# Transposing the gated FFN products by the DMA crossbar in 16-bit halves instead of on TensorE

## The chip, the cores and the metric

The kernel runs on one core of one Trainium2 chip. The metric is the device time of one execution in microseconds (us). A core has five engines with instruction streams of their own: TensorE (PE in the profile, with its weight loads as PEld), VectorE (DVE), ScalarE (ACT), GpSimd (POOL) and SyncE (SP), which here issues nearly all transfers. Sixteen DMA rings move the data.

## The reference

An encoder trunk of two layers on a sequence of 256 tokens with 1024 features in float32. Each layer is a half-step FFN, a mixing block with two attention branches, and a second half-step FFN:

```python
def swiglu(x, w_gate, w_up, w_down):
    return (jax.nn.silu(x @ w_gate) * (x @ w_up)) @ w_down

for l in range(DEPTH):                                   # 2
    x = x + 0.5 * swiglu(rms_norm(x, ffn1_norm[l]), ffn1_w_gate[l], ffn1_w_up[l], ffn1_w_down[l])
    ...                                                  # attention branches, gates, output projection
    x = x + 0.5 * swiglu(rms_norm(x, ffn2_norm[l]), ffn2_w_gate[l], ffn2_w_up[l], ffn2_w_down[l])
```

The hidden width D_FF is 2816. The change touches only the four FFNs: the gated product silu(x @ w_gate) * (x @ w_up) has tokens on the partitions when it is made, and must have the hidden features on the partitions to be multiplied by w_down.

## The kernel before

All 256 tokens stay on the chip, as two tiles of 128 tokens (t = 0 and 1). Every float32 product is made of three matmuls (`three`, lines 169 to 172): each operand is split by `split_to` (lines 183 to 185) into a high part, copied by ScalarE into a rounded format, and a low part, the difference, subtracted by VectorE; high times high, high times low and low times high are summed in PSUM.

**Weights.** SP loads them in pieces of 512 KB into four `raw` buffers (line 142, and line 348 for the down weights). ScalarE and VectorE split each piece into one of six pairs `wh`, `wl`, from which TensorE reads. A piece of an up stage serves four groups of three matmuls.

**The up stage of an FFN.** The hidden width is cut into eleven chunks of 256 columns (`for c in range(NFC)`). For each chunk four pieces of the gate and up weights are loaded, and for each of the two token tiles eight groups of three matmuls (`project`) fill a PSUM bank `g`, of which there are two: 256 columns of gate and 256 of up. Then `glu` (lines 440 to 445) applies silu on ScalarE (line 443) and multiplies on VectorE (line 444) into `hh`, a float32 tile of 128 tokens x 2 x 256. In some chunks (`PREP`, three in each FFN) `prepare` also loads two rows of down weights and forms their differences u and v, which it keeps in split form.

**The transposes.** Chunks are collected in pairs. A pair's `turn` (lines 315 to 322) is deferred until TensorE has done some more matmuls (`H_LAG`, `LAST_LAG`; `defer`, `tick` and `need` hold this list by hand), and then issues four transposes of 128x128 per chunk on TensorE through the identity, into a PSUM bank `tp` (line 320). `arrange` takes it from there. `PLAN` gives each chunk a letter. For S (three chunks), `split_to` reads PSUM and gives `hi` and `lo` of four blocks. For F and G (eight chunks), ScalarE copies PSUM to a tile `a` (line 330), VectorE forms four sums of blocks (line 333), and `split_to` gives seven blocks: these are the operands of a multiplication of 2x2 blocks with seven products in place of eight.

**The down stage.** `down` goes through the chunks in order: for F and G seven groups of three matmuls, whose weights are sums and differences of blocks (`differences`, line 352, unless prepared), for S eight. Chunk 0 comes first; chunks 9 and 10, both S, come last and together.

**Order.** TensorE's instructions are issued in the order of the program, which is fixed by hand with the deferrals. On the other engines and on SP's queue a planner fixes an order when the kernel is built, by priority (the order in the program) and by its own estimate of when each instruction becomes ready; on the chip each engine then follows that order and waits where something is not there.

**Buffers that the change shares.** Tag `xg` has two buffers, used by `hh` and by small tiles of the norms; tag `sums` has two of 4 KB per partition, used by `a`, by the differences `u` and `v`, and by the sums at the end of the down stage.

Of the kernel before, what the change touches and what calls it, by code (L numbers as in the profile page):

```python
# [11 lines left out]
F32 = mybir.dt.float32  # L12
F32R = mybir.dt.float32r
I32 = mybir.dt.int32
BF16 = mybir.dt.bfloat16
AF = mybir.ActivationFunctionType
ALU = mybir.AluOpType
AX = mybir.AxisListType
# [3 lines left out]
P = 128  # L22
# [4 lines left out]
T = S // P  # L27
KD = D // P
FC = 256
NFC = FF // FC  # L30
# [13 lines left out]
H_LAG, NORM_LAG, QK_LAG, P_LAG, V_LAG, M_LAG = 7.9, 4.0, 16, 10, 7.5, 5.5  # L44
LAST_LAG = 6.1
# [13 lines left out]
def hybrid_encoder(ctx, tc, x, w_gu1, w_d1, w_in, b_gate, qk_gain, rpb, sink, t5,  # L59
                   w_bna, w_bsw, w_out, w_gu2, w_d2, c_mask, c_band, out):  # L60
    nc = tc.nc
# [3 lines left out]
    act = ctx.enter_context(tc.tile_pool(name="act", bufs=1))  # L65
# [3 lines left out]
    ps_tp = ctx.enter_context(tc.tile_pool(name="ps_tp", bufs=2, space=PSUM))  # L69
# [18 lines left out]
    ident = const.tile([P, P], F32, name="ident")  # L88
# [5 lines left out]
    warm = const.tile([P, 1], F32, name="warm")  # L94
    warmed = nc.scalar.activation(warm, ident[:, :1], AF.Silu)
    qkg = const.tile([P, L, 4], F32, name="qkg")
# [27 lines left out]
    def linked(engine, emit):  # L124
        with ExitStack() as order:
            if engine in chain:
                order.enter_context(tc.issue_after(chain[engine].ins))
            inst = emit()
        if chain:
            chain[engine] = inst  # L130
        return inst
# [13 lines left out]
    def columns(w, l, c0, n, nk=KD):  # L145
        return [load(w[l, 2 * i * P:(2 * i + 2) * P, c0:c0 + n].rearrange("(k p) n -> p k n", p=P), 2, n)
                for i in range(nk // 2)]
# [7 lines left out]
    def defer(lag, key, fn):  # L155
        later.append((now[0] + lag, len(later), key, fn))
        later.sort(key=lambda e: e[0])

    def need(*keys):
        for e in [e for e in later if e[2] in keys]:  # L160
            later.remove(e)
            e[3]()
# [20 lines left out]
    def split_to(hi, lo, src):  # L183
        linked("act", lambda: nc.scalar.activation(hi, src, AF.Copy))  # L184
        linked("dve", lambda: nc.vector.tensor_tensor(lo, src, hi.bitcast(F32), ALU.subtract))  # L185
# [3 lines left out]
    rstd = [None] * T  # L189
# [3 lines left out]
    def norm(t, n, half, apart=False):  # L193
# [9 lines left out]
        if apart and half == 1:  # L203
            for i in range(4):
                linked("act", lambda: nc.scalar.activation(xg[:, i, :], tp[:, i, :], AF.Copy,
                                                           scale=gain[:, n, 4 + i:5 + i]))
# [7 lines left out]
    def square(t, half, junk=None):  # L214
        if junk is None:
            junk = act.tile([P, 512], BF16, name="junk", tag="xg", bufs=2)
        linked("act", lambda: nc.scalar.activation(junk, xs[t][:, half * 512:(half + 1) * 512], AF.Square,
                                                   accum_out=ssq[t][:, half:half + 1]))
# [6 lines left out]
    def opening(w, l, early):  # L225
        def piece(i, c=0):
            return load(w[l, 2 * i * P:(2 * i + 2) * P, c * 512:(c + 1) * 512].rearrange("(k p) n -> p k n", p=P),
                        2, 512)

        ps = [ps_g.tile([P, 512], F32, name="g", tag="g") for _ in range(T)]  # L230

        def steps(t, i):
            wh, wl = pieces[i]
            xh, xl = xT[t]
            for a, b in ((xh, wh), (xl, wh), (xh, wl)):
                for k in (2 * i, 2 * i + 1):
                    nc.tensor.matmul(ps[t], a[:, k, :], b[:, k % 2, :], start=a is xh and b is wh and k == 0,
                                     stop=b is wl and k == KD - 1)
            tick(2)

        pieces = []
        chain["act"] = warmed
        warmup(5)
        norm(0, 0, 0, True)
        pieces.append(piece(0))
        warmup(5)
        fetch(1, 0)
        norm(1, 0, 0, True)
        pieces.append(piece(1))
        fetch(0, 1)  # L250
        fetch(1, 1)
        warmup(3)
        steps(0, 0)
        norm(0, 0, 1, True)
        steps(1, 0)
        pieces.append(piece(2))
        norm(1, 0, 1, True)
        pieces.append(piece(3))
        square(0, 0, idle)
        square(0, 1, idle)  # L260
        for i in (1, 2, 3):
            for t in range(T):
                steps(t, i)
        second = [piece(0, 1)]
        square(1, 0, idle)
        early(ps[0])
        second.append(piece(1, 1))
        square(1, 1, idle)
        second += [piece(i, 1) for i in range(2, KD // 2)]
        chain.clear()  # L270
        defer(24, "constants", constants)
        defer(70, "scaled", scaled)
        return ps, second
# [36 lines left out]
    def ffn(l, n, w_gu, w_d, after):  # L310
        with tc.tile_pool(name="ffn", bufs=1) as fp:
            hs = {}
            SLOT = ((1, 2), (0, 3))

            def turn(group):
                tps = [ps_tp.tile([P, 4, P], F32, name="tp", tag="tp") for _ in group]
                for (_, hh), tp in zip(group, tps):
                    for t in range(T):
                        for i in range(2):
                            nc.tensor.transpose(tp[:, SLOT[t][i], :], hh[:, t, i * P:(i + 1) * P], ident)  # L320
                for (c, _), tp in zip(group, tps):
                    arrange(c, tp)

            def arrange(c, tp):
                m = 4 if PLAN[c] == "S" else 7
                hi = fp.tile([P, m, P], F32R, name=f"hi{m}", tag=f"hi{m}", bufs=NS if m == 7 else NFC - NS)
                lo = fp.tile([P, m, P], F32R, name=f"lo{m}", tag=f"lo{m}", bufs=NS if m == 7 else NFC - NS)
                if m == 7:
                    a = fp.tile([P, 8, P], F32, name="a", tag="sums", bufs=2)
                    nc.scalar.activation(a[:, :4, :], tp, AF.Copy)  # L330
                    for to, x, y, op in ((4, 0, 3, ALU.add), (6, 1, 0, ALU.subtract), (5, 4, 1, ALU.subtract),
                                         (7, 2, 5, ALU.subtract)):
                        nc.vector.tensor_tensor(a[:, to, :], a[:, x, :], a[:, y, :], op)
                    split_to(hi, lo, a[:, 1:, :])
                else:
                    with tc.high_priority(150 if c == NFC - 1 else 0):
                        split_to(hi, lo, tp)
                hs[c] = (hi, lo)

            def get(t, k):  # L340
                need(("h", k // 2))
                return [h[:, SLOT[t][k % 2], :] for h in hs[k // 2]]

            stored = {}
# [68 lines left out]
            def combine(acc):  # L413
                p1, p16 = [fp.tile([P, 2, 512], F32, name=n, tag="sums", bufs=2) for n in ("p1", "p16")]
                ends = act.tile([P, 512], F32, name="ends", tag="xg", bufs=2)
                nc.scalar.activation(p1[:, 0, :], acc["1"], AF.Copy, scale=0.5)

# [20 lines left out]

            def glu(t, ps, pair):
                if t == 0:  # L440
                    pair[0] = act.tile([P, T, FC], F32, name="hh", tag="xg", bufs=2)
                sg = fp.tile([P, FC], F32, name="sg", tag="sg", bufs=2)
                linked("act", lambda: nc.scalar.activation(sg, ps[:, :FC], AF.Silu, scale=rstd[t]))  # L443
                linked("dve", lambda: nc.vector.scalar_tensor_tensor(pair[0][:, t], ps[:, FC:], rstd[t], sg,  # L444
                                                                     op0=ALU.mult, op1=ALU.mult))

            waiting = []
            for c in range(NFC):
                first = n == 0 and c == 0
                pair = [None]  # L450
                if first:
                    both, second = opening(w_gu, l, lambda ps: glu(0, ps, pair))
                elif n == 0 and c == 1:
                    pieces = second
                else:
                    pieces = columns(w_gu, l, c * 512, 512)
                prep = PREP if n else PREP_FIRST
                if c in prep:
                    prepare(prep[c])
                for t in range(T):  # L460
                    if not first:
                        glu(t, project(t, pieces, 512), pair)
                    elif t:
                        glu(t, both[t], pair)
                waiting.append((c, pair[0]))
                if c % 2 or c == NFC - 1:
                    defer(LAST_LAG if c == NFC - 1 else H_LAG, ("h", c), lambda group=waiting: turn(group))
                    waiting = []

            down()  # L470

# [373 lines left out]
```

## Time and profile before

| | |
|---|---|
| time, median of 3 runs | 1077.5 us (1076.47 to 1078.26) |
| span of the profiled execution, first to last instruction | 1075.2 us; its own whole time is not listed apart from the three runs |
| granted clock of TensorE, mean | 0.999 |
| TensorE busy | 1068.2 us (99%), 5125 instructions |
| VectorE busy | 875.8 us (81%) |
| ScalarE busy | 671.5 us (62%) |
| GpSimd busy | 116.7 us (11%) |
| DMA | 212.63 MB, 198 GB/s in the mean |

The profile's rows read as follows. A group of instructions has its source line, engine and operation, the tile written and those read, the shape and the count; then the busy time in us and the mean of one in ns; then the time for which the engine stood idle just before them, and what ended that. A row of waits has who waited for whom, the total in us, how many times, and the longest. A window has start and end, its length, then busy time (and number of instructions) of PE, PEld, DVE, ACT and POOL, the granted clock, the DMA rings' busy share and GB/s. A DMA row has the tile, the queue, the count, the size and the median time from issue to landing. Busy times of matmuls overlap at their ends, so a chain of work or the distance between starts tells better what one costs.

### The profile page before, as it was taken

Reading aid. Unit: us, or ns where it says so; the run is one execution under the profiler, and the core shown is the slowest. Engines: PE = TensorE matmul, PEld = TensorE weight load, DVE = VectorE, ACT = ScalarE, POOL = GpSimd, SP = SyncE. Lnnn points to the kernel's source line nnn. Section 1 sums busy time; section 2 is a strip of 40 time slices with the busy share of each in tenths; the row PEclk is TensorE's granted clock in tenths of the full one; section 3 lists DMA queues with packets and bytes.
Section 4 is the critical chain, followed back from the end, with each engine's and each line's share of the span. In section 5 each row is a group of like instructions: output and inputs, shape, how many; then the busy total and the mean of one; then the engine's idle time right before and its main releaser. Section 6 shows DMA issues by size and latency. Waiting matters only on the chain.

```text
span 1075.2 us, 14749 instructions
## 1 busy us (share of the span) xinstructions
PE 1068.2 (99%) x5125; PEld 890.3 (83%) x5125; DVE 875.8 (81%) x1337; ACT 671.5 (62%) x1014; POOL 116.7 (11%) x118
## 2 busy tenths in 40 slices
PE   8999999999999999999999999999999999999998
PEld 6888888888888888888888888888888888888887
DVE  6678799889886768869977887988898867778696
ACT  6566654788764556565565665557877646566552
POOL 1000120243520000000000000003534000000000
PEclk9999999999999999999999999999999999999999
DMA  7767656765654667756657765657666554776652
GB/s 247 227 214 237 215 190 191 228 194 155 192 188 137 198 199 246 242 168 191 214 162 238 227 213 185 199 153 247 177 195 185 176 175 160 237 231 203 188 196 89
DMA packets 98827, 212.63 MB, mean 198 GB/s; under 512 B 7568, under 2 KB 13744, under 8 KB 98752
## 3 DMA queue, kind: packets, MB, share of 16 engines
q1 hardware_dynamic: 98560, 211.60, 62.3%
q8 instruction: 40, 0.66, 0.2%
q14 instruction: 35, 0.29, 0.1%
q0 software_dynamic: 192, 0.08, 0.1%
HBM read 210.59 MB, written 1.06 MB: 197 GB/s over the span
## 4 chain that ended last, share of the span: by engine, by line
PE 97%; DMA 1%; ACT 1%; DVE 0%; issue 0%; SPq 0%; ACTq 0%
PE g L170 22%; PE g L172 22%; PE g L171 22%; PE acc L170 5%; PE acc L172 5%; PE acc L171 5%; PE tp L320 2%; PE sc L568 1%; PE po L603 1%; PE tp L170 1%; PE tp L171 1%; PE tp L172 1%; PE pt L589 1%; PE tp L201 1%; PE br L170 1%; PE br L171 1%
## 5 line engine op out<-in xcount | busy, mean ns | idle before, releaser
L185 DVE TENSOR_TENSOR wl<-raw,wh 128x1024 fp32r<-128x1024 f32 x336 | 405.7, 1219 | 65.5 <-ACT wh L184 61.8
L184 ACT ACTIVATE wh<-raw 128x1024 fp32r<-128x1024 f32 x336 | 346.7, 1045 | 117.3 <-DMA raw<-in_w_gu 51.4
L170 PE MATMUL g<-wh,xh 128*128 128x512 f32 (+1 forms) x976 | 383.1, 393 | 0.5 <-DVE hh L444 0.5
L172 PE MATMUL g<-wh,xl 128*128 128x512 f32 (+1 forms) x976 | 377.8, 387 | 0.0
L171 PE MATMUL g<-wl,xh 128*128 128x512 f32 (+1 forms) x976 | 377.5, 387 | 0.0
L172 PEld LDWEIGHTS g<-wh,xl 128*128 128x128 f32 x976 | 183.4, 188 | 39.1 <-DVE xl L185 1.5
L170 PEld LDWEIGHTS g<-wh,xh 128*128 128x128 f32 x976 | 183.6, 188 | 33.8 <-DVE hh L444 1.1
L171 PEld LDWEIGHTS g<-wl,xh 128*128 128x128 f32 x976 | 183.7, 188 | 33.4 <-DVE wl L185 0.6
L443 ACT ACTIVATE sg<-g,rs_y 128x256 f32<-128x256 f32 x88 | 41.1, 467 | 89.7 <-PE g L172 77.3
L444 DVE SCALAR_TENSOR_TENSOR hh<-g,rs_y,sg 128x256 f32<-128x256 f32 x88 | 42.3, 481 | 53.0 <-ACT sg L443 53.0
L170 PE MATMUL acc<-wh,hi 128*128 128x512 f32 x180 | 71.2, 395 | 0.0
L171 PE MATMUL acc<-wl,hi 128*128 128x512 f32 x180 | 70.2, 390 | 0.0
L172 PE MATMUL acc<-wh,lo 128*128 128x512 f32 x180 | 70.1, 390 | 0.0
L176 POOL TENSOR_TENSOR rs_y<-ms,mhalf 128x1 f32<-128x1 f32 x12 | 8.1, 678 | 556.5 <-DVE ms L222 548.0
L352 DVE TENSOR_TENSOR u<-raw 128x512 f32<-128x512 f32 x64 | 41.7, 686 | 20.9 <-DMA raw<-in_w_d 20.8
L184 ACT ACTIVATE corner<-raw 128x512 fp32r<-128x512 f32 x32 | 20.1, 629 | 40.4 <-DMA raw<-in_w_d 22.4
L581 POOL TENSOR_TENSOR S<-S,sm 128x512 f32<-128x512 f32 x32 | 37.2, 1161 | 65.6 <-DVE sm L580 38.3
L172 PEld LDWEIGHTS acc<-wh,lo 128*128 128x128 f32 x180 | 33.8, 188 | 7.2
L171 PEld LDWEIGHTS acc<-wl,hi 128*128 128x128 f32 x180 | 33.8, 188 | 6.7
L170 PEld LDWEIGHTS acc<-wh,hi 128*128 128x128 f32 x180 | 33.8, 188 | 6.7
L184 ACT ACTIVATE wh<-v 128x1024 fp32r<-128x1024 f32 x20 | 21.2, 1062 | 28.9 <-DVE v L352 24.5
L574 ACT ACTIVATE S<-S,mx 128x256 f32<-128x256 f32 x64 | 31.9, 499 | 8.0 <-DVE mx L571 7.9
(189 smaller groups left out, 1522.0 us busy)
## 6 DMA issues: line engine op xcount, KB each, us to landing
raw<-in_w_gu SPq DMA_DIRECT2D x176, 512.0 KB, 4.5
raw<-in_w_d SPq DMA_DIRECT2D x100, 512.0 KB, 4.2
raw<-in_w_in SPq DMA_DIRECT2D x64, 512.0 KB, 4.7
raw<-in_w_out SPq DMA_DIRECT2D x16, 512.0 KB, 3.6
bb<-in_b_gate SPq DMA_DIRECT2D x16, 256.0 KB, 3.6
raw<-in_w_bsw SPq DMA_DIRECT2D x8, 512.0 KB, 3.9
raw<-in_w_bna SPq DMA_DIRECT2D x8, 512.0 KB, 3.5
raw<-in_w_d SPq DMA_DIRECT2D x12, 256.0 KB, 2.7
```

Source lines behind the costliest of these rows:

```text
L170: nc.tensor.matmul(ps, xh, wh, start=first, stop=False)
L171: nc.tensor.matmul(ps, xh, wl, start=False, stop=False)
L172: nc.tensor.matmul(ps, xl, wh, start=False, stop=last)
L184: linked("act", lambda: nc.scalar.activation(hi, src, AF.Copy))
L185: linked("dve", lambda: nc.vector.tensor_tensor(lo, src, hi.bitcast(F32), ALU.subtract))
L201: nc.tensor.transpose(tp[:, i, :], xs[t][:, k * P:(k + 1) * P], ident)
L320: nc.tensor.transpose(tp[:, SLOT[t][i], :], hh[:, t, i * P:(i + 1) * P], ident)
L352: sub = lambda to, x, y: nc.vector.tensor_tensor(to, x, y, ALU.subtract)
L443: linked("act", lambda: nc.scalar.activation(sg, ps[:, :FC], AF.Silu, scale=rstd[t]))
L444: linked("dve", lambda: nc.vector.scalar_tensor_tensor(pair[0][:, t], ps[:, FC:], rstd[t], sg, op0=ALU.mult, op1=ALU.mult))
L574: nc.scalar.activation(S_[:, t, :], S_[:, t, :], AF.Exp, bias=mx[:, t:t + 1], scale=-1.0, accum_out=sm[:, t:t + 1])
L581: nc.gpsimd.tensor_tensor(S_, S_, sm.unsqueeze(2).to_broadcast([P, T, S]), ALU.mult)
```

## The change

Per chunk, right after its second gated product, without pairing or deferral:

1. `glu` writes its product in the order of the four blocks that the down stage wants (`hh` is 128 x 4 x 128).
2. ScalarE reads `hh` as 16-bit halves and copies them into a tile `z16` so that all low halves stand first and then all high halves (1024 values of 16 bits per partition).
3. One crossbar transpose on SP's queue turns `z16` into `zT`, eight blocks of 128x128 16-bit values, in a `sums` buffer.
4. ScalarE copies `zT` into `a` (a second `sums` buffer) so that the halves are side by side again as float32.
5. For F and G the four sums and the split follow as before; for S the split now reads `a`.

TensorE's transposes, their PSUM banks and the copy of line 330 go, and so do the deferrals of `turn`. The call of `high_priority` for the last chunk's split goes too.

```diff
-            def turn(group):
-                tps = [ps_tp.tile([P, 4, P], F32, name="tp", tag="tp") for _ in group]
-                for (_, hh), tp in zip(group, tps):
-                    for t in range(T):
-                        for i in range(2):
-                            nc.tensor.transpose(tp[:, SLOT[t][i], :], hh[:, t, i * P:(i + 1) * P], ident)
-                for (c, _), tp in zip(group, tps):
-                    arrange(c, tp)
-
-            def arrange(c, tp):
+            def turn(c, hh):
+                z = act.tile([P, 2, 4 * P], U16, name="z16", tag="xg", bufs=2)
+                nc.scalar.activation(z, hh.bitcast(U16).rearrange("p s (n two) -> p two (s n)", two=2), AF.Copy)
                 m = 4 if PLAN[c] == "S" else 7
                 hi = fp.tile([P, m, P], F32R, name=f"hi{m}", tag=f"hi{m}", bufs=NS if m == 7 else NFC - NS)
                 lo = fp.tile([P, m, P], F32R, name=f"lo{m}", tag=f"lo{m}", bufs=NS if m == 7 else NFC - NS)
+                zT = fp.tile([P, 2 * 4, P], U16, name="zT", tag="sums", bufs=2)
+                nc.sync.dma_start_transpose(zT, z.rearrange("p two n -> p (two n)"))
+                a = fp.tile([P, 8, P], F32, name="a", tag="sums", bufs=2)
+                nc.scalar.activation(a[:, :4, :].bitcast(U16).rearrange("p s (n two) -> p two (s n)", two=2),
+                                     zT.rearrange("p (two s) n -> p two (s n)", two=2), AF.Copy)
                 if m == 7:
-                    a = fp.tile([P, 8, P], F32, name="a", tag="sums", bufs=2)
-                    nc.scalar.activation(a[:, :4, :], tp, AF.Copy)
                     for to, x, y, op in ((4, 0, 3, ALU.add), (6, 1, 0, ALU.subtract), (5, 4, 1, ALU.subtract),
                                          (7, 2, 5, ALU.subtract)):
                         nc.vector.tensor_tensor(a[:, to, :], a[:, x, :], a[:, y, :], op)
                     split_to(hi, lo, a[:, 1:, :])
                 else:
-                    with tc.high_priority(150 if c == NFC - 1 else 0):
-                        split_to(hi, lo, tp)
+                    split_to(hi, lo, a[:, :4, :])
                 hs[c] = (hi, lo)
 
             def get(t, k):
-                need(("h", k // 2))
                 return [h[:, SLOT[t][k % 2], :] for h in hs[k // 2]]
...
                 if t == 0:
-                    pair[0] = act.tile([P, T, FC], F32, name="hh", tag="xg", bufs=2)
+                    pair[0] = act.tile([P, 4, P], F32, name="hh", tag="xg", bufs=2)
+                h = pair[0][:, 0::3, :] if t else pair[0][:, 1:3, :]
...
-                waiting.append((c, pair[0]))
-                if c % 2 or c == NFC - 1:
-                    defer(LAST_LAG if c == NFC - 1 else H_LAG, ("h", c), lambda group=waiting: turn(group))
-                    waiting = []
+                turn(c, pair[0])
```

More of the change, by code (lines that the diff above doesn't have):

```diff
@@ L15 @@
 BF16 = mybir.dt.bfloat16
+U16 = mybir.dt.uint16
 AF = mybir.ActivationFunctionType
@@ L440, in glu @@
                 if t == 0:
-                    pair[0] = act.tile([P, T, FC], F32, name="hh", tag="xg", bufs=2)
+                    pair[0] = act.tile([P, 4, P], F32, name="hh", tag="xg", bufs=2)
+                h = pair[0][:, 0::3, :] if t else pair[0][:, 1:3, :]
                 sg = fp.tile([P, FC], F32, name="sg", tag="sg", bufs=2)
                 linked("act", lambda: nc.scalar.activation(sg, ps[:, :FC], AF.Silu, scale=rstd[t]))
-                linked("dve", lambda: nc.vector.scalar_tensor_tensor(pair[0][:, t], ps[:, FC:], rstd[t], sg,
-                                                                     op0=ALU.mult, op1=ALU.mult))
-            waiting = []
+                linked("dve", lambda: nc.vector.scalar_tensor_tensor(
+                    h, ps[:, FC:].rearrange("p (i n) -> p i n", i=2), rstd[t], sg.rearrange("p (i n) -> p i n", i=2),
+                    op0=ALU.mult, op1=ALU.mult))
             for c in range(NFC):
@@ L464, in ffn @@
                         glu(t, both[t], pair)
-                waiting.append((c, pair[0]))
-                if c % 2 or c == NFC - 1:
-                    defer(LAST_LAG if c == NFC - 1 else H_LAG, ("h", c), lambda group=waiting: turn(group))
-                    waiting = []
+                turn(c, pair[0])
             down()
```

## The prediction

> **What bounds the kernel now.** I read the page's busy shares first, then its chain of work that ended last, then TensorE's waits, to see whether TensorE is busy because it works or because it is fed late.
>
> ```profile
> span 1075.2 us, 14749 instructions
> PE 1068.2 (99%) x5125; PEld 890.3 (83%) x5125; DVE 875.8 (81%) x1337; ACT 671.5 (62%) x1014; POOL 116.7 (11%) x118
> ...
> PE 97%; DMA 1%; ACT 1%; DVE 0%; issue 0%; SPq 0%; ACTq 0%
> PE g L170 22%; PE g L172 22%; PE g L171 22%; PE acc L170 5%; PE acc L172 5%; PE acc L171 5%; PE tp L320 2%; PE sc L568 1%; PE po L603 1%; PE tp L170 1%; PE tp L171 1%; PE tp L172 1%; PE pt L589 1%; PE tp L201 1%; PE br L170 1%; PE br L171 1%
> ```
>
> ```profile
> PE idle L120 <- DVE blank L115: 1.6, 1, 1.6
> PE tp L201 <- DMA x<-in_x: 1.3, 1, 1.3
> PE g L170 <- DVE hh L444: 0.5, 1, 0.5
> ```
>
> The chain is 97% TensorE, and TensorE waits for others 3.4 us in all, at the opening. So TensorE's own instructions are the time, and each one taken away is worth its place in the stream. Line 320, the transposes that the change takes off TensorE, has 2% of that chain. What has to be judged is whether the other engines and the queue, which now just hide, still hide. Their room is read from the four stages of gate and up projections (24 to 129, 365 to 480, 546 to 661 and 896 to 1011 us), from a prepared chunk inside one (421 to 433) and from one down stage (480 to 542).
>
> ```profile
> core 0: us, PE busy (x) PEld busy (x) DVE busy (x) ACT busy (x) POOL busy (x), PEclk, DMA share, GB/s
> 24.00:129.00 105.00, 104.54 (x478) 86.57 (x478) 81.89 (x115) 63.06 (x79) 2.52 (x5) 1.00 0.71 231
> 365.00:480.00 115.00, 115.00 (x528) 95.31 (x527) 85.68 (x120) 69.14 (x88) 0.56 (x1) 1.00 0.68 221
> 480.00:542.00 62.00, 62.00 (x282) 51.19 (x281) 58.44 (x78) 35.50 (x45) 0.55 (x1) 1.00 0.56 179
> 546.00:661.00 115.00, 114.96 (x528) 95.30 (x527) 87.25 (x121) 67.66 (x87) 0.93 (x1) 1.00 0.69 222
> 896.00:1011.00 115.00, 115.00 (x528) 95.26 (x528) 85.97 (x120) 68.65 (x88) 0.56 (x1) 1.00 0.69 220
> ...
> 421.00:433.00 12.00, 12.00 (x55) 9.94 (x54) 10.50 (x11) 7.17 (x9) 0.00 (x0) 1.00 0.92 301
> ```
>
> In the gate and up stages ScalarE is busy about 60% and the DMA rings 0.68 to 0.71; in the down stage VectorE has 58.44 of 62 us. Those are the three covers that the change leans on.
>
> **The change, part by part.** First, what goes from TensorE. The chain in order of time shows the transposes as pieces of their own:
>
> ```profile
> 456.20 0.87 PE tp L320 x8
> 478.85 0.87 PE tp L320 x8
> 489.95 0.44 PE tp L320 x4
> ```
>
> A pair of chunks with its eight transposes takes 22.65 us (478.85 less 456.20). It has 96 matmuls of 512 columns, so a matmul takes (22.65 - 0.87)/96 = 0.227 us of the stream and a group of three 0.68. One of the four FFNs has 44 transposes, five groups of eight and one of four: 5 x 0.87 + 0.44 = 4.79 us, and four FFNs 19.2 us. I take the pieces of the chain, not the busy time of the group below (23.1 us), for that counts ends that overlap the next matmul. A chunk's period goes from 11.33 to 10.89 us; that is the budget for everything else.
>
> ```profile
> L320 PE MATMUL tp<-ident,hh 128*128 128x128 f32 x176 | 23.1, 272 | 0.0
> L184 ACT ACTIVATE wh<-raw 128x1024 fp32r<-128x1024 f32 x328 | 342.1, 1055 | 116.7 <-DMA raw<-in_w_gu 51.4 <-PE g L172 37.4 <-PE acc L172 11.6
> L330 ACT ACTIVATE a<-tp 128x512 f32<-128x512 f32 x32 | 17.9, 593 | 0.0
> L443 ACT ACTIVATE sg<-g,rs_y 128x256 f32<-128x256 f32 x88 | 41.1, 467 | 89.7 <-PE g L172 77.3 <-issue 12.0 <-PE g L237 0.3
> L444 DVE SCALAR_TENSOR_TENSOR hh<-g,rs_y,sg 128x256 f32<-128x256 f32 x88 | 42.3, 481 | 53.0 <-ACT sg L443 53.0
> L184 ACT ACTIVATE hi<-tp 128x512 fp32r<-128x512 f32 x12 | 7.2, 597 | 1.0 <-PE tp L320 1.0
> ```
>
> ScalarE gets two copies per chunk, one that separates 1024 halves per partition and one that joins them. The nearest row by elements is the weight split of 1024 values, 1.055 us. No row reads or writes 16-bit values at a stride: I bound one copy by 0.6 us (512 words, the L330 row) and by 2.1 us (twice the split), and take 1.055, whose element count it has. It loses the 593 ns copy on the 32 chunks of plans F and G. Net 44 x 2.11 - 32 x 0.593 = 73.9 us, 1.68 per chunk. Now ScalarE has 69.14 x 11.33/115 = 6.81 us of work in a chunk's period; it will have 8.49 of 10.89, and 2.4 us stay free. With the upper bound it would have 10.6, still under the period but with nothing left for waits. VectorE keeps the same instructions: the gated products go to another layout in the same 128x256 size, and the low halves of the three S chunks read SBUF in place of PSUM. I cost that at nothing; VectorE's free quarter in the up stages is the cover.
>
> The rings and SP. Each chunk adds one transpose of 256 KB between parts of SBUF, 44 in all, on SP's queue among the weight loads.
>
> ```profile
> q1 hardware_dynamic: 98560, 211.60, 62.3%
> ...
> q0 software_dynamic: 192, 0.08, 0.1%
> ...
> raw<-in_w_gu SPq DMA_DIRECT2D x176, 512.0 KB, 4.5
> raw<-in_w_d SPq DMA_DIRECT2D x100, 512.0 KB, 4.2
> raw<-in_w_in SPq DMA_DIRECT2D x64, 512.0 KB, 4.7
> ...
> raw<-in_w_d SPq DMA_DIRECT2D x12, 256.0 KB, 2.7
> ...
> raw<-in_w_in SPq DMA_DIRECT2D x8, 256.0 KB, 3.8
> ```
>
> Ring time now: 0.69 x 11.33 = 7.8 us per chunk, so 10.89 leaves 3.1. A load's packet is 211.60 MB/98560 = 2147 bytes and takes 0.623 x 1075.2 x 16/98560 = 0.109 us of one ring. Lower end: the transpose at the same rate per byte is 262144/2147 = 122 packets, 0.83 us of all sixteen rings. Upper end: a row of 128 two-byte values is 256 bytes, so 1024 rows, each at the full 0.109 us (the q0 row, 0.1% for 192 packets of some 420 bytes, says that a short packet is hardly cheaper), 7.0 us. I take 1.5 us, what 512 KB costs more to landing than 256 KB of the same tensor (4.2 against 2.7), because the byte count is the same; then the rings are 9.3 of 10.89 us busy and the loads still hide. The Trainium skill, "DMA: Bandwidth & Descriptors", section "Latency and other measured facts", has crossbar transposes at 261 GB/s in one kernel, which by estimate is 1.0 us here; the sum by it is the same, and no run before shows it.
>
> ```profile
> SPq L142 <- DVE wl L185: 437.1, 195, 8.3
> ...
> L142 SPq DMA_DIRECT2D raw<-in_w_gu x176: 367/368/567, 1.2 to 995.4; - x176
> ...
> ACT wh L184 <- DMA raw<-in_w_gu: 51.4, 51, 2.4
> ```
>
> SP issues a load in 0.37 us and mostly stands waiting for a raw buffer. The transpose's issue lies between 0.33 and, at four times as many rows, 1.5 us: hidden. But it waits in SP's order for ScalarE's first copy, with the next weight loads queued behind it, and itself stands behind loads that wait for a buffer. Behind those loads wait ScalarE's splits, then TensorE; the cover is the six pairs of weight buffers, each worth 4 x 0.68 = 2.72 us of TensorE. Loads that are late already stop ScalarE by at most 2.4 us and TensorE never, so I cost this at nothing; uncovered, it costs what the rival on ScalarE's order costs.
>
> The path of one chunk: silu 0.47, product 0.48, separation 1.06, transpose 2.7 to 3.8 to landing, joining 1.06, then the high and low parts. It ends some 9 us after the chunk's last matmul. Nothing in the up stage reads it; the down stage starts with chunk 0 and comes to chunks 9 and 10 last. The latency itself is hidden. The banks that the transposes used on TensorE come free earlier; that earns nothing, as TensorE never waits for them. What the path holds are two buffers "sums", shared with the differences of the down weights, and two "xg". For xg, the separation ends 2.0 us after the chunk and the next product comes 5.4 us after it: hidden. For "sums" the last chunk counts. The timelines of VectorE and then of TensorE at the start of the second down stage, which begins at 485.02:
>
> ```profile
> 480.91 0.69 DVE L352 TENSOR_TENSOR u<-raw 128x512 f32<-128x512 f32 x1 [4.78 <-DMA raw<-in_w_d]
> ...
> 491.27 0.68 DVE L352 TENSOR_TENSOR v<-raw,u 128x512 f32<-128x512 f32 x1
> ...
> 494.40 1.22 DVE L185 TENSOR_TENSOR wl<-v,wh 128x1024 fp32r<-128x1024 f32 x1
> ```
>
> ```profile
> 485.02 0.39 PE L170 MATMUL acc<-wh,hi 128*128 128x512 f32 x1
> ...
> 498.43 0.39 PE L170 MATMUL g<-wh,hi 128*128 128x512 f32 x1
> ```
>
> The first difference v that is not prepared is split by 495.62 and used at 498.43, 2.8 us early, with VectorE nearly full. If the halves of chunk 10 and their sums hold both buffers until about 8.2 us after the stage begins (2.0 + 3.8 + 1.06, a high part of 0.6 and a low part of 0.7), v follows with two subtractions of 0.69 and a split of 1.06 and 1.22: 11.9 us, against 13.0 when it is due (13.4 less the 0.44 of transposes that are gone). It fits, by 1.1 us, if nothing else delays it. Ends: 0 and 3 us a stage; I take 1, since VectorE's queue there is full and the row that this is nearest to has only 2.8 us to spare. Four stages make 4 us.
>
> Sum: the span 1075.2 - 19.2 + 4 = 1060.0. The profiled execution's own time isn't listed; the median of the runs, 1077.5, stands 2.3 us over its span, which I keep: 1062.3, so 1062.
>
> **The rivals.** One, on the other side: the transposes hold the rings. Each takes r us of all rings; from r = 11.33 - 7.8 = 3.5 us on, an up stage takes longer than now. At the upper end of 7.0 a chunk takes 14.8, 3.5 more than now, and 44 chunks 154 us: 1232. For it: rows of 256 bytes are far shorter than any load here, and the prepared chunk above already fills the rings to 0.92. Against: both sides lie in SBUF, and the rate per byte of the loads leaves 0.83. The Trainium skill speaks against the change here: "VectorE: DVE Perf Modes", section "The three transpose paths", gives 390 ns on TensorE and 1309 ns by the crossbar for 128x128 of bf16, and its rules keep TensorE where PSUM will do. Eight blocks one after another would by estimate be 10.5 us, and the sum some 1385; the trace has TensorE's transpose at 0.109 us of the stream (0.87 by eight), less than that page, and shows nothing of the crossbar.
>
> Two: ScalarE stands still before the joining copy. Its instructions run in a fixed order; if the join stands right behind the separation it waits the whole landing, 2.7 to 3.8 us, with splits and the next silu behind it. Free are 2.4 us per chunk, and break-even with now lies at 2.4 + 0.44 = 2.84. At a stall of 3.8 the period is 12.29, and 44 x 0.96 = 42 us more: 1120. With half of the 3.8 spent on other work in between, a chunk stalls 1.9; then only the twelve prepared chunks overrun, which have two more splits of 1.06 and so 0.9 free where the others have 3.0 (the 2.4 is their mean): 12 x 1.0 us on 1058.3, 1070. For: SP often stands for a buffer, up to 8.3 us, so that a transpose can come later than its order supposes. Against: ScalarE waited 77.3 us for TensorE before the silu, so it runs ahead.
>
> Three: the "sums" buffers come late by the whole bound of 3 us at each down stage, and VectorE, 94% busy, doesn't catch up: 1058.3 + 12 = 1070.
>
> **How the numbers follow.** The forecast, 1057 to 1068, has 0.51: TensorE bound before and after, all three covers hold by rows. The rings 0.15 (all slower, 0.12 of it over 1100). ScalarE's order 0.24: 0.07 still faster, 0.05 the same, 0.12 slower, 0.04 of it over 1100. The buffers 0.10: 0.07 faster, 0.02 the same, 0.01 slower. Sum: faster 0.65, same 0.07, slower 0.28, where 0.2% (2.2 us) is about what this measurement tells from no change. The range from 1056 to 1100 leaves out 0.16 above and some 0.03 below.
>
> **What would show it.** Right: line 320 gone, the chain still 97% TensorE, pairs of chunks at 21.8 us, ScalarE near 745 us, the two copies near 1.05 us each, DMA share in the up stages near 0.83, TensorE's waits under 6 us. Wrong by the rings: DMA share over 0.95 and splits that wait for loads. Wrong by ScalarE's order: long waits of the join for the transpose, then of TensorE for splits or of a projection for a bank. Wrong by the buffers: TensorE waits 10 to 15 us into the down stages for split differences. A transpose that lands much later than 4 us, or a half-word copy of 2 us, would upset the sum most.

## The result, and the profile after

The changed kernel takes 1141.2 us (median of four runs, 1140.04 to 1141.82) against 1077.6 before (median of four; the three above gave 1077.5): 5.9% longer, ratio 1.059 with a 95% interval of 1.0575 to 1.0605. The forecast was 1062, faster. In the profiles below line numbers have moved: the split is now L185 and L186, the groups of three L171 to L173, the separating copy L318, the transfer L323, the joining copy L325, the silu L439 and the product L440.

The page after, its shares and the chain that ended last:

```profile
span 1139.8 us, 14538 instructions
...
PE 1082.4 (95%) x4949; PEld 877.2 (77%) x4949; DVE 877.7 (77%) x1337; ACT 745.8 (65%) x1070; POOL 113.7 (10%) x118
...
PE 33%; DMA 24%; DVE 21%; ACT 12%; issue 9%; SPq 0%; ACTq 0%; POOL 0%; DVEq 0%; POOLq 0%
DMA raw<-in_w_gu 11%; DVE wl L186 11%; DMA zT<-z 8%; PE g L171 6%; PE g L172 6%; PE g L173 6%; ACT wh L185 5%; ACT a L325 3%; DMA raw<-in_w_d 3%; DVE u L347 2%; DVE v L347 2%; ACT z L318 2%; PE acc L172 2%; PE acc L173 2%; PE acc L171 2%
```

Before, 97% of the chain was TensorE. Now it is 33%, and the chain runs through weight loads, splits, the transfer and the joining copy: nobody is full (ScalarE 65%, VectorE 77%, TensorE 95% by a busy time that now also holds the ends of matmuls that nothing overlaps), and each waits for another. TensorE's own waits, which were 3.4 us, are now 53; the longest rows:

```profile
PE g L171 <- DVE hh L440: 18.8, 15, 2.4
PE g L172 <- DVE wl L186: 16.7, 20, 1.3
PE tp L171 <- ACT wh L185: 6.3, 4, 3.1
PE g L171 <- ACT wh L185: 4.5, 8, 1.0
```

It waits for a PSUM bank whose product is late (hh), and for weights whose split is late (wl, wh). Behind both stand waits that were smaller before (the first two 66.6 and 51.4 us) or absent:

```profile
DVE wl L186 <- ACT wh L185: 104.4, 110, 4.4
ACT wh L185 <- DMA raw<-in_w_gu: 82.6, 59, 3.2
ACT a L325 <- DMA zT<-z: 47.9, 20, 5.6
...
DVE a L330 <- ACT a L325: 35.3, 16, 6.9
```

The new costs, by shape, and the transfers:

```profile
L325 ACT ACTIVATE a<-zT 128x1024 uint16<-128x1024 uint16 x44 | 60.2, 1369 | 48.9 <-DMA zT<-z 47.9
L318 ACT ACTIVATE z<-hh 128x1024 uint16<-128x1024 uint16 x44 | 46.3, 1052 | 23.6 <-DVE hh L440 23.6
...
q1 hardware_dynamic: 145024, 223.14, 66.7%
...
zT<-z SPq DMA_TRANSPOSE x44, 3.9
```

The windows of an up stage and of a down stage, to set beside those of before:

```profile
398.00:511.00 113.00, 107.19 (x453) 84.93 (x452) 81.24 (x116) 78.18 (x90) 0.00 (x0) 0.98 0.78 225
...
515.30:578.40 63.10, 59.39 (x254) 47.17 (x253) 55.02 (x70) 34.63 (x44) 0.55 (x1) 0.97 0.55 175
```

From the starts of the matmuls in the trace, the four down stages, 55 to 57 us each before, take 65.7, 63.1, 64.6 and 60.7 us: 30 us more in all. The rest of the 65 us of span, 34 us, lies ahead of and between them, where x1_relief, the kernel below that has TensorE's relief alone, is 18 us shorter than before.

One place shows the pattern. ScalarE, and then VectorE, in an up stage:

```profile
408.91 1.05 ACT L185 ACTIVATE wh<-raw 128x1024 fp32r<-128x1024 f32 x1
410.72 1.06 ACT L318 ACTIVATE z<-hh 128x1024 uint16<-128x1024 uint16 x1 [0.76 <-DVE hh L440]
417.38 1.34 ACT L325 ACTIVATE a<-zT 128x1024 uint16<-128x1024 uint16 x1 [5.59 <-DMA zT<-z]
418.59 0.44 ACT L439 ACTIVATE sg<-g,rs_y 128x256 f32<-128x256 f32 x1
418.93 1.04 ACT L185 ACTIVATE wh<-raw 128x1024 fp32r<-128x1024 f32 x1
```

```profile
410.61 1.21 DVE L186 TENSOR_TENSOR wl<-raw,wh 128x1024 fp32r<-128x1024 f32 x1
418.75 0.69 DVE L330 TENSOR_TENSOR a<-a 128x128 f32<-128x128 f32 x3 [6.93 <-ACT a L325]
419.36 0.48 DVE L440 SCALAR_TENSOR_TENSOR hh<-g,rs_y,sg 128x256 f32<-128x256 f32 x1
```

Here the join stands right behind the separation in ScalarE's fixed order. The transfer lands 5.6 us later; until then ScalarE does nothing, although the next silu and splits are queued behind the join; VectorE has the sums next and stands 6.9 us. This is the plainest case: in the median chunk 3.0 us of other work of ScalarE lies between separation and join, and the transfer lands 4.0 us after the separation. TensorE at the same place, and its window from 419.9 on:

```profile
417.25 0.39 PE L173 MATMUL g<-wh,xl 128*128 128x512 f32 x1
419.90 0.80 PE L171 MATMUL g<-wh,xh 128*128 128x512 f32 x1 [2.25 <-DVE hh L440]
420.49 0.63 PE L172 MATMUL g<-wl,xh 128*128 128x512 f32 x1
420.91 0.63 PE L173 MATMUL g<-wh,xl 128*128 128x512 f32 x1
```

```profile
419.90:422.60 2.70, 2.70 (x6) 2.17 (x7) 2.70 (x4) 2.33 (x4) 0.00 (x0) 0.50 0.15 19
```

The silu behind the join and the product behind the sums come late, so the bank comes free late and TensorE stands 2.25 us. Then it runs slower: the granted clock is 0.50, and matmuls start 0.59 and then 0.42 to 0.43 us apart, where they start 0.227 apart otherwise. The change has seven such spells, 34 us in all, which cost up to 16 us; before has none but at its very end. Each begins at or within 5 us after TensorE idled for 1.9 to 3.1 us, and kernels in which TensorE waits more have on the whole a lower mean clock: 0.999 with 3 us of waits (before), 0.998 with 22 (y6_forced below), 0.988 with 47 (x4_own), 0.985 with 53 here, 0.961 with 99 (y1_actq). So lateness is paid for twice. No run varies the clock alone, and the prediction had no term for it.

### The profile page after: what moved, and what is told of

Its sections match the earlier page's. It is cut to its first block, busy times and chain, and to the rows that moved or that the text cites. A ratio compares the mean times of both kernels' runs of the same rounds, so it can differ in the third digit from the quotient of the medians.

```text
span 1139.8 us, 14538 instructions
## 1 busy us (share of the span) xinstructions
PE 1082.4 (95%) x4949; PEld 877.2 (77%) x4949; DVE 877.7 (77%) x1337; ACT 745.8 (65%) x1070; POOL 113.7 (10%) x118
## 3 DMA queue, kind: packets, MB, share of 16 engines
HBM read 210.59 MB, written 1.06 MB: 186 GB/s over the span
## 4 chain that ended last, share of the span: by engine, by line
PE 33%; DMA 24%; DVE 21%; ACT 12%; issue 9%; SPq 0%; ACTq 0%; POOL 0%; DVEq 0%; POOLq 0%
DMA raw<-in_w_gu 11%; DVE wl L186 11%; DMA zT<-z 8%; PE g L171 6%; PE g L172 6%; PE g L173 6%; ACT wh L185 5%; ACT a L325 3%; DMA raw<-in_w_d 3%; DVE u L347 2%; DVE v L347 2%; ACT z L318 2%; PE acc L172 2%; PE acc L173 2%; PE acc L171 2%
## 5 line engine op out<-in xcount | busy, mean ns | idle before, releaser
L186 DVE TENSOR_TENSOR wl<-raw,wh 128x1024 fp32r<-128x1024 f32 x336 | 405.0, 1219 | 100.4 <-ACT wh L185 99.5
L185 ACT ACTIVATE wh<-raw 128x1024 fp32r<-128x1024 f32 x336 | 344.1, 1041 | 125.3 <-DMA raw<-in_w_gu 82.6
L171 PE MATMUL g<-wh,xh 128*128 128x512 f32 (+1 forms) x976 | 387.0, 396 | 20.0 <-DVE hh L440 18.8
L172 PE MATMUL g<-wl,xh 128*128 128x512 f32 (+1 forms) x976 | 381.7, 391 | 13.9 <-DVE wl L186 13.9
L173 PE MATMUL g<-wh,xl 128*128 128x512 f32 (+1 forms) x976 | 379.7, 389 | 0.0
L171 PEld LDWEIGHTS g<-wh,xh 128*128 128x128 f32 x976 | 184.6, 189 | 65.7 <-DVE hh L440 27.8
L173 PEld LDWEIGHTS g<-wh,xl 128*128 128x128 f32 x976 | 184.4, 189 | 38.9 <-DVE xl L186 1.0
L325 ACT ACTIVATE a<-zT 128x1024 uint16<-128x1024 uint16 x44 | 60.2, 1369 | 48.9 <-DMA zT<-z 47.9
L171 PE MATMUL acc<-wh,hi 128*128 128x512 f32 x180 | 71.7, 398 | 0.0
L173 PE MATMUL acc<-wh,lo 128*128 128x512 f32 x180 | 71.1, 395 | 0.0
L318 ACT ACTIVATE z<-hh 128x1024 uint16<-128x1024 uint16 x44 | 46.3, 1052 | 23.6 <-DVE hh L440 23.6
L330 DVE TENSOR_TENSOR a<-a 128x128 f32<-128x128 f32 x128 | 32.6, 286 | 36.1 <-ACT a L325 35.3
L440 DVE SCALAR_TENSOR_TENSOR hh<-g,rs_y,sg 128x256 f32<-128x256 f32 x88 | 42.1, 478 | 20.5 <-ACT sg L439 20.4
L186 DVE TENSOR_TENSOR lo<-a,hi 128x896 fp32r<-128x896 f32 (+1 forms) x44 | 43.0, 977 | 12.1 <-ACT hi L185 11.9
L185 ACT ACTIVATE wh<-v 128x1024 fp32r<-128x1024 f32 x20 | 21.2, 1059 | 38.0 <-DVE v L347 35.4
L185 ACT ACTIVATE corner<-raw 128x512 fp32r<-128x512 f32 x32 | 20.0, 626 | 38.5 <-DMA raw<-in_w_d 35.4
L439 ACT ACTIVATE sg<-g,rs_y 128x256 f32<-128x256 f32 x88 | 40.0, 455 | 3.2 <-PE g L173 2.9
```

The source lines that it names most:

```text
L171: nc.tensor.matmul(ps, xh, wh, start=first, stop=False)
L172: nc.tensor.matmul(ps, xh, wl, start=False, stop=False)
L173: nc.tensor.matmul(ps, xl, wh, start=False, stop=last)
L318: nc.scalar.activation(z, hh.bitcast(U16).rearrange("p s (n two) -> p two (s n)", two=2), AF.Copy)
L325: nc.scalar.activation(a[:, :4, :].bitcast(U16).rearrange("p s (n two) -> p two (s n)", two=2), zT.rearrange("p (two s) n -> p two (s n)", ...
L440: linked("dve", lambda: nc.vector.scalar_tensor_tensor(h, ps[:, FC:].rearrange("p (i n) -> p i n", i=2), rstd[t], sg.rearrange("p (i n) -> ...
```

## The experiments

Theories: **order** (ScalarE, and VectorE behind it, stand at the join because the order fixed when the kernel is built puts it where the transfer has not landed); **queue** (the transfer waits in SP's order for the separated halves, with weight loads behind it); **buffers** (zT and a hold both "sums"); **work** (the copies fill ScalarE); **crossbar** (the transfer holds the rings). Where one time is given, it is one run; before, run beside it on the same chip, took 1076.5 to 1077.6. Four runs of one kernel lie up to 2 us apart, so a difference of 2 or 3 us between single runs decides nothing.

**What the relief is worth.** x1_relief drops separation, transfer and join:

```diff
-nc.scalar.activation(z, <halves of hh>, AF.Copy); zT = ...; nc.sync.dma_start_transpose(zT, z)
-nc.scalar.activation(<halves of a>, zT, AF.Copy)
+if m == 7: nc.scalar.activation(a[:, :4, :], hh, AF.Copy)     # S chunks: split_to(hi, lo, hh)
```

> Leaves out the transposition itself: no separation, no crossbar transfer; the sums read the gated products as they are (one 593 ns copy on F and G chunks, the split straight from the products on S chunks). It is the change with TensorE's relief alone. If TensorE's 19.2 us were real room, all theories expect 1077.5 - 19.2 = 1058, within 1056 to 1064. If it stays above 1070, TensorE's place was not free time, and what was lost lies in the order of the other engines, not in the new work.

1057.35 us: 19.2 us less than before beside it (1076.54), what the chain's pieces gave. The first term of the sum is right.

**The copies without the transfer.** x2_copies has both copies, and the join reads z:

```diff
-zT = fp.tile(...); nc.sync.dma_start_transpose(zT, ...); <join reads zT>
+<join reads z>
```

> Keeps both of ScalarE's half-word copies, leaves out the crossbar transfer and its buffer zT: the joining copy reads the separated halves directly (so nothing is transposed). Theory of ScalarE's work (74 to 88 us more in copies are too much): stays at 1120 or more. Theory of the buffers (zT and the joined tile hold both 'sums' buffers while the prepared and first differences wait) and theory of ScalarE's order (it stands at the join for the landing): both fall to 1058 to 1075, since the path is short and one buffer is enough.

1068.1: the copies cost 10.8 us where they were put down at nothing, yet alone they leave a gain of 8. The theory of work falls as the main cause; 73 us come with the transfer.

**The crossbar.** x3_plain:

```diff
-nc.sync.dma_start_transpose(zT, z.rearrange("p two n -> p (two n)"))
+nc.sync.dma_start(zT, z.rearrange("p two (s n) -> p (two s) n", s=4))
```

> The crossbar transpose is replaced by an ordinary transfer of the same 256 KB from z to zT, same place in SP's queue, same buffers and waits (nothing is transposed). Theory of the crossbar (its 1056 short packets hold the rings or SP's 1.2 us of issue): falls below 1090. Theories of the buffers and of ScalarE's order: a plain landing of 2.7 to 3.8 us is about as late as the crossbar's 3.9, so 1125 to 1142.

1129.6: an ordinary transfer is nearly as bad. 11.6 us belong to the crossbar, the rest to having a transfer there at all.

**The buffers.** x4_own:

```diff
-zT = fp.tile([P, 2 * 4, P], U16, name="zT", tag="sums", bufs=2)
+zT = fp.tile([P, 2 * 4, P], U16, name="zT", tag="zT", bufs=1)      # and silu writes into hh in place
```

> The change with a buffer of its own for zT (one of 2 KB), paid for by writing silu's output into the product's tile in place; 'sums' is then left to the joined tile and the differences, as before. Theory of the buffers: at least half of what was lost against 1058 comes back, 1060 to 1100. Theory of ScalarE's order and of its work: 1125 to 1145.

1135.3: 5.9 us, not half. The standing grew instead (rows below).

**The queue.** y1_actq issues the transpose with nc.scalar.dma_start_transpose; y3_pool the plain transfer of x3 with nc.gpsimd.dma_start:

> The same change with the crossbar transpose issued from ScalarE's queue, right behind the separating copy, instead of from SP's. Theory of the queue (a transfer waits in SP's order for the separated halves, 78 us in all, with weight loads behind it): at least half of the 73 us over the copies alone (1068) comes back, 1070 to 1105. Theory of ScalarE's order (it stands at the joining copy for the landing, 48 us, and runs the rest late): 1120 to 1145, or more by ScalarE's own issue of 44 x 1.2 us.

> As x3_plain (an ordinary transfer in the crossbar's place, nothing transposed, 1130), but issued from GpSimd's queue, so that SP has only its loads. Theory of the queue: 1070 to 1100. Theory of ScalarE's order: 1120 to 1145.

1213.5 and 1135.2. Freeing SP of the transfer gains nothing (y3 against 1129.6 of x3), which speaks against the queue as the main cause. It doesn't settle it: from GpSimd the transfer landed after 5.0 us in the median, from SP in x3 after 3.3, so a gain on SP's queue could be hidden by the later landing. From ScalarE's own queue it is far worse, above both ranges; the tile's view has the issue, the landing and the wait there:

```profile
L323 ACTq DMA_TRANSPOSE zT<-z x44: 1247/1248/1345, 28.8 to 1152.7; - x44
...
  DMA zT<-z: 132.6, 38
...
DMA to landing us min/median/max: 2.7/5.5/12.6
```

**The order, first try.** y2_late calls the join 12 groups later in the program, with zT's own buffer; y4_actlate does so with the transpose on ScalarE's queue:

```diff
+defer(12, ("h", c), lambda: arrange(c, zT))     # arrange: join, sums, split
```

> Transfer still from SP, zT in its own buffer as in x4_own (1135), but the joining copy and all behind it are called 12 groups of three matmuls later in the program (some 8 us), so that splits and silus of the next chunk come before it in ScalarE's order. Theory of ScalarE's order: the wait for zT goes below 15 us and the time to 1068 to 1095. Theory of the queue: 1115 to 1140.

> y1 and y2 together: crossbar from ScalarE's queue, zT's own buffer, join 12 groups later. If queue and order are the two causes and add up: 1060 to 1085. If neither is: above 1115.

1142.4 and 1204.2. By the expectation y2 would speak against the order. But the wait for zT had not gone, it had grown to 98 us: for these engines a later call is only a lower priority, and the planner left the join where it was. In the trace of y2_late 1.5 us of other work of ScalarE lie between separation and join in the median, as in x4_own. The edit did not do what it should, so y2 and y4 decide nothing.

**The order, forced.** y6_forced ties the join behind the second silu of the next chunk, so that a whole chunk of other work lies between:

```diff
+with tc.issue_after(silu[0].ins):               # second silu of chunk c + 1
     nc.scalar.activation(<halves of a>, zT, AF.Copy)
```

> Copies stay on ScalarE, zT has its own buffer, and the joining copy of a chunk is tied behind the second silu of the next chunk, a whole chunk later, in ScalarE's fixed order (y2's later call had not moved it: there ScalarE waited 98 us for zT). Theory of ScalarE's standing: its wait for zT goes to nearly 0 in the up stages and the time to 1068 to 1090 (x2, copies without transfer, 1068, plus the wait at the last chunk). Theory of the queue or of the buffers: above 1115.

1087.4, 47.8 us below x4_own, from which it differs only in the place of the join and of the sums and split that follow it. z2_half ties the join behind the first silu of the next chunk:

> y6_forced with the joining copy tied behind the first silu of the next chunk in place of the second: about half as far behind the separation. In y6 the transfer landed 4.5 us (median) behind the separation and the join began at 7.3. Theory of standing in a fixed order: part of the wait comes back, 20 to 60 us of waits for zT and 1095 to 1130. If only the own buffer or the call's place in the program had helped, not the distance: within 5 us of 1087.

1144.1, and 97 us of waits: worse than both expectations. In the median the tie leaves 1.5 us of other work between separation and join, no more than x4_own has, against 5.0 in y6_forced; so it is not half the distance, and the two expected ranges are not tested as they were meant. What z2 does show is that neither the own buffer nor the tie as such helps without work in between. The waits of the join for the transfer, in this order: the change, x4_own, y2_late, z2_half, y6_forced and z1_lastlate; each from its own list of waits:

```profile
ACT a L325 <- DMA zT<-z: 47.9, 20, 5.6
```

```profile
ACT a L325 <- DMA zT<-z: 66.8, 37, 5.4
```

```profile
ACT a L328 <- DMA zT<-z: 98.3, 39, 5.4
```

```profile
ACT a L333 <- DMA zT<-z: 96.6, 40, 4.7
```

```profile
ACT a L333 <- DMA zT<-z: 3.9, 5, 1.8
```

```profile
ACT a L335 <- DMA zT<-z: 0.4, 1, 0.4
```

The first four kernels take 1135 to 1144 us, the last two 1087 and 1072. In the trace of z2_half the join begins 4.25 us (median) behind the separation, with the landing at 4.17; in y6_forced at 7.3, with the landing at 4.5. SP still stands 89 us before its transfers in y6_forced, against 96 in x4_own and 78 in the change, and yet the time came back: with y3 that rules the queue out as the main cause.

**The last chunk.** z1_lastlate is y6_forced with chunk 10's join tied behind the splits of chunk 4 in the down stage:

```diff
+                    if c == 5:
+                        silu[0] = last_act[0]           # the last split issued so far, of chunk 4
+                        arrange(*pend.pop(0))           # chunk 10: the join tied behind it, then the split
```

> y6_forced (1087) with the last chunk's joining copy tied into the down stage behind the splits of chunk 4 there, since chunk 10 is needed last. Of y6's 30 us over x1 (1057) some 18 lie in the down stages. If the last chunk's chain causes them: 1072 to 1081, about the time of before. If they come from the queue or from the differences alone: 1084 to 1090.

1072.0 (1070.98 to 1073.03), ratio to before 0.9949, interval 0.9932 to 0.9967: 0.5% shorter than before. The second down stage, in y6_forced and here:

```profile
488.40:548.90 60.50, 57.66 (x254) 46.03 (x253) 53.17 (x69) 34.72 (x43) 0.55 (x1) 1.00 0.57 182
```

```profile
482.80:539.60 56.80, 56.39 (x254) 46.24 (x253) 53.58 (x69) 34.42 (x43) 0.55 (x1) 1.00 0.60 194
```

63.1 us in the change, 60.5 in y6_forced, 56.8 here; all four together 254, 240 and 226 us, against 224 before. The last chunk's chain at the head of the down stage was the rest of what was lost there.

**What the crossbar still costs.** z3_plain exchanges z1's transpose for the plain transfer, and x5_inplace tests the silu in place on x1_relief:

> z1_lastlate (1072) with an ordinary transfer of 256 KB in the crossbar's place (nothing is transposed). In the change's own order that exchange was worth 11 us (1141 to 1130). If the crossbar costs by its landing alone, it is hidden here: within 3 us of 1072. If it costs by holding the rings against the loads or by SP's 1.2 us of issue: 5 us or more below, 1061 to 1067.

> x1_relief (1057, transposition left out) with silu written into the product's tile in place, which x4, y2, y6 and z1 also have to make room for zT's own buffer. If that is neutral, as all theories take it: 1056 to 1060.

1063.0 and 1060.0. With its landing covered the crossbar keeps 9.0 us of its own; which of its issue and its ring time makes them was not separated. Rows of z1_lastlate and then z3_plain:

```profile
q1 hardware_dynamic: 145024, 223.14, 69.6%
...
L324 SPq DMA_TRANSPOSE zT<-z x44: 1237/1238/2035, 28.2 to 1017.1; - x44
```

```profile
q1 hardware_dynamic: 104896, 223.14, 65.2%
...
L324 SPq DMA_DIRECT2D zT<-z x44: 470/471/526, 29.0 to 1007.3; - x44
```

x5_inplace is 2.7 us above x1_relief, but on another chip, where before took 1.1 us more (1077.6 against 1076.5). That the silu in place costs anything is not shown; if it does, x4's 5.9 us are a net figure.

**GpSimd.** p1_pool moves both copies to nc.gpsimd.tensor_copy, p2_pooljoin the join alone, p3_poolown is p1 with zT's own buffer:

> The change with both half-word copies on GpSimd in place of ScalarE; transfer, queue and buffers stay. GpSimd's copies may take some 2 us each, and it is idle in the FFNs. Theory of ScalarE (its two copies and its standing at the join delay splits and silus): 1060 to 1075, faster than before. Theory of the buffers or of the transfer on SP's queue: 1110 to 1140, since the path only gets longer.

> Only the joining copy goes to GpSimd; ScalarE keeps the separation. ScalarE then waits for no transfer but keeps 46 us of the 106 us of copies. Theory of ScalarE's standing: 1065 to 1085; theory of its work: about half way between the change (1141) and p1. If p1 and this both stay over 1110, ScalarE is not the cause.

> p1 with zT in a buffer of its own (silu in place, as in x4_own). If the 'sums' buffers matter once ScalarE is free of the copies, 3 to 15 us below p1; otherwise within 3 us of it.

1191.3, 1146.5 and 1139.5: p1 and p2 are misses for the theory of ScalarE as it stood there, and p3 lies 52 us below p1, far more than expected of zT's own buffer. By the expectation of p2, ScalarE would then not be the cause; what remains is that the standing had only moved. The waits of p3_poolown suggest why taking the join away did not free ScalarE: it then stood for what follows the join, and for loads.

```profile
ACT wh L185 <- DMA raw<-in_w_gu: 106.9, 78, 3.8
...
ACT hi L185 <- DVE a L330: 45.7, 19, 4.5
...
ACT hi L185 <- POOL a L325: 11.6, 5, 4.2
```

p4_pooltied keeps GpSimd's join and ties the sums and the split behind the next chunk's second silu:

> As y6_forced, but the joining copy is on GpSimd, and what follows it (sums and split) is tied behind the second silu of the next chunk. If p2 (1146) and p3 (1139) were slow because ScalarE and VectorE then stood at the sums and the split in place of the join: 1075 to 1095. If GpSimd's copy itself (VectorE slowed beside it, transfers held back) was the cause: above 1115.

1108.9, between the two expectations. It is 37.6 us below p2_pooljoin, from which it differs by the tie and by zT's own buffer (what each gives was not separated), and 21.5 us over y6_forced. VectorE's busy time is 907.4 us there against 881.5 in y6_forced, so it is slower beside GpSimd's copies; that this is the whole of it was not shown, and neither the 1191 of p1 nor its distance from p3 is explained.

## Why the prediction was wrong

**TensorE's relief, 19.2 us:** right (x1_relief, 19.2).

**ScalarE, 2.4 us free per chunk:** this is the step that failed; the sum put ScalarE's order at nothing. The work was near: the separation 1.052 us against 1.055, the join 1.369 against 1.055. That the total came to 745.8 us against 745 forecast is luck: the two copies take 106.5 us, not 92.8, and the busy time rose less than that mostly because instructions that overlap at their ends count once. The mistake was in the wait. I took free time in the mean over a chunk as room for waits. x2_copies shows that the work alone costs 10.8 us though it fits, and the join's wait in the change, 47.9 us over 44 chunks, is 1.1 us each, under the 2.84 at which I put break-even. By that reckoning nothing was lost to before. In a fixed order the wait comes at one place: behind it stand the silu that frees a PSUM bank and the splits, and VectorE stands as well (35.3 us at the sums); raw buffers come free later and so do loads (82.6 us of waits against 51.4). The rival named the right mechanism with 0.24, and its signs, waits of the join, then of TensorE for splits and for a bank, are the rows above; but it priced it by the mean, 1120 at a stall of 3.8. The runs put the order, with the last chunk's part and the lower clock, at 63.3 us (x4_own 1135.3 less z1_lastlate 1072.0). That 1120 lies 58 us above the forecast, near this, is luck: the mean stall was 1.1, not 3.8.

**The path of one chunk, "the latency itself is hidden":** right by data, wrong by order. Nothing in the up stage reads the result, but ScalarE and VectorE carried its steps in line ahead of work that TensorE needed. y6_forced hides the same latency by moving the join and what follows it.

**Buffers "sums", 1 us a stage, 3 at most:** x4_own puts the buffer alone at 5.9 us, near the forecast's 4. The down stages lost 30 us, though, and z1_lastlate shows that they lost much of it to the last chunk's chain, 15.4 us after y6_forced. My check of that place, 11.9 us against 13.0 due, let the steps follow each other at once, and looked at v alone. In the trace of the change the first difference u, which began 4.1 us ahead of the second down stage before, starts 10.2 us into it, when the join ends; by my figures the join would end at 6.9 (2.0 + 3.8 + 1.06). The shared buffer is not all of that: in x4_own, where zT has its own, u starts at 10.2 too; in y6_forced it starts at 7.2 and in z1_lastlate at 0.8.

**SP's queue, at nothing:** right as to the main loss (y3_pool and y6_forced together); a small part isn't excluded. For the issue I had 0.33 to 1.5, and it was 1.23 us.

**The rings, 1.5 us a transpose:** measured by the shares of q1, (0.667 x 1139.8 - 0.623 x 1075.2)/44 = 2.05 us, between the ends and far from the 3.5 that decide; up-stage share 0.78, forecast 0.83. The upper end had the packets of 256 bytes at 0.109 us each; in the trace they take 0.029 in the mean, so the q0 row misled. The transfer is not free: 9.0 us in z3_plain's exchange, 11.6 in x3_plain's. The Trainium skill's 261 GB/s ("DMA: Bandwidth & Descriptors", section "Latency and other measured facts") would by estimate be 1.0 us; the trace does not agree, 2.05 us of ring time beside the weight loads are 128 GB/s. By the Trainium skill's 1309 ns per block ("VectorE: DVE Perf Modes", section "The three transpose paths"), eight in a row would by estimate be 10.5 us; the trace does not agree, with 3.9 us in the median and 2.7 at least to the landing of all eight.

From the change to the relief, step by step: 1141.2, own buffer 1135.3, join a chunk later 1087.4, last join later still 1072.0, plain transfer 1063.0, no copies, no transfer and no ties 1060.0 (x5_inplace). Order makes 63 of the 81 us. The last step, 3 us for both copies and a plain transfer, is less than the 10.8 us of the copies alone in x2_copies, where the join mostly follows the separation at once; so part of what x2 puts down to work may be order too.

## What to carry to other kernels

A step that leaves a full engine for a longer path must be followed instruction by instruction through the fixed order of every engine that it now passes: mean free time on an engine is no cover for a wait, since what stands behind the wait may be what the bottleneck needs next. Tie the far end of a transfer behind a piece of other work that takes longer than its landing (in y6_forced 5.0 us of other work in the median, so that the join began at 7.3 us and the landing at 4.5 was past), and read the wait of that one instruction afterwards: a later call in the program may leave it where it was. With that, and a buffer of its own for what is transferred, the same change went from 5.9% slower to 0.5% faster.

## What was not expected of the hardware

ScalarE's half-word copy cost 1.052 us when it read at a stride of two halves and 1.369 when it wrote so. One crossbar transpose of 256 KB took 1056 packets (46464 more on q1 over 44) and 1.23 us of SP's issue, a plain copy of the same bytes 144 and 0.47; issued from ScalarE's queue it took 1.25 us there and landed after 5.5 us in the median against 3.9. And a wait cost TensorE more than its length: in the spells with a granted clock of 0.50, some 3 to 10 us each, matmuls started 0.43 us apart instead of 0.227.
